# Feature-major products with hi and lo activations as one 512-column operand, halves summed in evacuation, one pool of eight PSUM banks

## The chip, the cores and the metric

The kernel runs on one core of one Trainium2 chip. The metric is the time of one execution on the device in microseconds. Three timed runs of the kernel before gave 1062.16, 1062.8 and 1064.5 us, so the median is 1062.8 us. The profile is of one more execution; the profiler's span, from its first to its last instruction, is 1060.4 us.

## The reference, cut to what matters

Two layers over 256 tokens of width 2048, in float32. Layer 0 is stick-breaking attention, layer 1 multi-head latent attention on keys and values made once from the residual stream.

```
# every layer: h = RMSNorm(x); y = W_out(mixer(h) * silu(gate(h))); x += RMSNorm(y)
#              x += (p[i] @ W_ple) * sigmoid(x @ W_gate)

def mixer_a(h, w_in, w_out):                       # 16 heads of 128
    q, k, v, g = jnp.split(h @ w_in, 4, axis=-1)   # w_in 2048 x 8192
    o = stick_breaking_attention(heads(q), heads(k), heads(v))
    return (o * jax.nn.silu(g)) @ w_out

def shared_kv(x, ...):                             # latent of 512, rotary key of 64
    ckv, k_rope = split(rms_norm(x) @ w_dkv); ckv = rms_norm(ckv)
    k_nope, v = ckv @ w_uk, ckv @ w_uv

def mixer_b(h, kv, w_in, ...):
    cq, g = jnp.split(h @ w_in, [512], axis=-1)    # g is 2048 wide
    q = rms_norm(cq) @ w_uq                        # per head 128 + 64 rotary
    return (mla_attention(q, k, v) * jax.nn.silu(g)) @ w_out
```

## The kernel before

Every product is done in float32r in two parts: an operand is split into `hi` (its float32r rounding, made by ScalarE, `split` and `split_gain`, lines 82 and 86) and `lo` (the rest, made by VectorE, lines 83 and 87). A product is the sum hi*hi + hi*lo + lo*hi, added up in PSUM; `mm3` (lines 108 to 111) issues these three matrix instructions.

Weights come in units of half a MiB (`unit`, line 89): one DMA into a `raw` buffer [128, 1024], then `whi` on ScalarE and `wlo` on VectorE. There are four buffers of each of the three.

There are two shapes of product. `rows` (token-major) keeps a 128-token block of the activations stationary and streams 512 columns of weights. `cols` (feature-major) keeps a 128x128 block of weights stationary and streams the activations of all 256 tokens. Per weight block and per 128 rows of the contraction, `cols` issues three instructions of 256 columns: `whi` with the activations' hi (L109), `whi` with their lo (L110), `wlo` with their hi (L111). Two blocks share a PSUM bank of 512 columns, the left and the right half.

Feature-major are the gates of mixer A (four groups of four heads, `gate_group` and the three groups written out ahead of it), queries and keys of mixer A (`group_a`, four groups each), the gates of mixer B (four groups) and the nope keys and queries of mixer B (`group_b`, on the latents `latT`, two units for each of both in each of four groups). A group of the first three kinds is 8 units of 8 (row block, weight block) steps, in two banks; a unit of the last kind is 8 such steps, in one bank.

A result leaves PSUM in one operation per bank: VectorE multiplies a bank by the row of 1/rms (`gate_out` line 221, `group_a` line 337), or copies it (`group_b` line 550). The gates then pass through ScalarE's Silu (line 223).

PSUM has eight banks. The pool has two tags: `acc`, four banks for the large products, and `att`, four banks for attention, transposes and the row of 1/rms (one gate group uses two of them as well).

The order on each engine is made when the kernel is built: a scheduler takes the program in the order in which it is written and orders the ready instructions of each engine. The attention of a group of heads is woven into the weight stream of the next group (`weave`): a head has three stages, two units apart. An engine then works through its own list in order.

`actT` tiles hold activations as [hi or lo, row block, token], so that hi and lo of one row block lie 16 KB apart. `latT` holds the two latents in the same way.

Of the kernel before, what the change touches and what calls it, by code (L numbers as in the profile page):

```python
# [46 lines left out]
def hybrid_trunk(ctx: ExitStack, tc: tile.TileContext, a: dict):  # L47
    """Token-major residual; activations that feed a product are kept feature-major, split into two
    float32r parts (hi + lo is the float32 value exactly). A product is hi*hi + hi*lo + lo*hi,
    summed in PSUM in float32."""  # L50
# [8 lines left out]
    def acc():  # L59
        return psum.tile([P, SLAB], F32, tag="acc", name="acc", bufs=4)  # L60

    def att():
        return psum.tile([P, SLAB], F32, tag="att", name="att", bufs=4)
# [5 lines left out]
    # ---------------------------------------------------------------- residual stream  # L69
# [10 lines left out]
    # ---------------------------------------------------------------- weights  # L80
# [8 lines left out]
    def unit(src, n=UNIT, gains=None, parts=1):  # L89
        """Half a MiB of weights, split; gains: a factor per row, for each equal part of the columns."""  # L90
# [45 lines left out]
    def weave(stream, jobs, at):  # L136
        """Runs the stream of weight units; the stages of jobs[i] come after at[i], at[i] + LAG, ... of them."""
# [9 lines left out]
    # ---------------------------------------------------------------- constants  # L147
# [37 lines left out]
    def rstd_of(ssq, n, name):  # L185
        """ssq [P, NT, m] -> (mean + eps) ** -0.5, [P, NT]."""
# [10 lines left out]
    def rstd_row(r):  # L197
        """[P, NT] per token -> the same row in every partition, twice: [P, 2, T]."""
# [13 lines left out]
    def gate_group(g, aT, sg, get, row):  # L212
        o = [acc(), acc()]
        for u in range(8):
            cols(o, aT, get(u), 2 * u, 2, GRP, NK)
        gate_out(g, o, sg, row)
# [20 lines left out]
    o0, o1 = [acc(), acc()], [acc(), acc()]  # L237
    warm_up(WARM)
    for u in range(8):
# [4 lines left out]
        cols(o0, hT, w, 2 * u, 2, GRP, NK)  # L244
# [3 lines left out]
    c2 = tmp.tile([P, 2 * P + CHUNK], F32, tag="e", name="c2", bufs=2)  # L248
    for u in range(8):
        cols(o1, hT, unit_ga(1, u), 2 * u, 2, GRP, NK)  # L250
# [5 lines left out]
    o2 = [att(), att()]  # L256
    for u in range(8):
        cols(o2, hT, unit_ga(2, u), 2 * u, 2, GRP, NK)
# [4 lines left out]
        if u == 4:  # L263
            rstd0 = rstd_of(ssq0, D, "rstd0")
            rrow0 = rstd_row(rstd0)
            gate_out(0, o0, sgA, rrow0)
            gate_out(1, o1, sgA, rrow0)
    gate_out(2, o2, sgA, rrow0)
# [13 lines left out]
    gate_group(3, hT, sgA, lambda u: unit_ga(3, u), rrow0)  # L282

    # ---------------------------------------------------------------- mixer A
# [6 lines left out]
    def finish_head(h, o, sg, yT):  # L291
        y = tmp.tile([P, T], F32, tag="t256", name="y", bufs=2)
# [3 lines left out]
    def weighted_v(v, hh, w):  # L296
        """o.T [d, t] = v.T @ w.T; w [key, (t over keys 0..127 | last t tile over keys 128..255)]."""
# [32 lines left out]
    def group_a(g, q, k, v):  # L330
        for dst, base, row in ((k, NG, rrow0), (q, 0, rrow0q)):
            o = [acc(), acc()]
            for u in range(8):
                cols(o, hT, unit(a["w_in_a"][(base + g) * 8 + u]), 2 * u, 2, GRP, NK)
# [338 lines left out]
```

## Time and profile before

| | before |
|---|---|
| median of 3 runs | 1062.8 us (1062.16 to 1064.5) |
| span of the profiled execution, first to last instruction | 1060.4 us |
| TensorE busy | 1052.8 us, 6699 matrix instructions |
| VectorE busy | 606.7 us, 823 instructions |
| ScalarE busy | 536.2 us, 780 instructions |
| DMA | 189.17 MB, 178 GB/s on the mean |
| granted TensorE clock | 0.999 of full speed |

A time is that of a whole execution; the profiled execution's own time, by the profile, is its span, and the median of the timed runs lies 2.4 us above it. "Busy" of TensorE is the union of its instructions' modelled intervals. Those intervals overlap: one 256-column instruction is shown 0.28 us long while the next one starts 0.12 us after it, so a sum of shown durations is no time, and what an instruction costs is read from one start to the next. Weight loads (PEld) run beside the instructions. On the other engines a shown duration is close to the step from one instruction to the next.

### The profile page before, as it was taken

The numbers are of one execution on the slowest core, as the hardware profiler recorded it, in microseconds if no ns is written. First come the engines' busy times: TensorE is split into PE (matmuls) and PEld (weight loads), VectorE is DVE, ScalarE is ACT, GpSimd is POOL, SyncE is SP. The second block draws the span as 40 slices with busy tenths as digits, with TensorE's granted clock in tenths as the row PEclk, the third lists the DMA queues.
The fourth block names the chain that finished last, engine by engine and source line by source line (L and its number), as shares of the span: only waits on it lengthen the run. The fifth ranks groups of instructions, "written<-read, shape, count | busy, mean of one in ns | idle before, by whom it ended". The sixth has DMA issues, their size and how long they took to land.

```text
span 1060.4 us, 16605 instructions
## 1 busy us (share of the span) xinstructions
PE 1052.8 (99%) x6699; PEld 952.9 (90%) x6699; DVE 606.7 (57%) x823; ACT 536.2 (51%) x780; POOL 6.8 (1%) x10
## 2 busy tenths in 40 slices
PE   8999999999999999999999999999999999999998
PEld 7999999989989988888888999999988978888888
DVE  7454444554545555556666575555676755558554
ACT  7544335445445446545555555555454454446442
POOL 0000000000000000000000000000000000000000
PEclk9999999999999999999999999999999999999999
DMA  8755555555555554564756476656533334665662
GB/s 329 281 176 182 180 185 182 169 162 174 162 163 174 171 179 149 178 207 145 225 178 188 130 245 194 181 183 191 172 119 121 120 120 139 205 184 193 210 212 79
DMA packets 55821, 189.17 MB, mean 178 GB/s; under 512 B 6208, under 2 KB 6976, under 8 KB 55744
## 3 DMA queue, kind: packets, MB, share of 16 engines
q1 hardware_dynamic: 55600, 188.09, 56.5%
q8 instruction: 52, 0.85, 0.3%
q14 instruction: 25, 0.20, 0.1%
q10 hardware_dynamic: 144, 0.02, 0.0%
HBM read 185.99 MB, written 2.10 MB: 177 GB/s over the span
## 4 chain that ended last, share of the span: by engine, by line
PE 98%; DMA 1%; DVE 0%; ACT 0%; SPq 0%; issue 0%
PE acc L109 29%; PE acc L111 29%; PE acc L110 29%; PE att L300 1%; PE att L110 1%; PE att L111 1%; PE att L109 1%; PE att L171 1%; PE att L301 1%; PE att L523 1%; PE att L519 1%; PE att L308 1%; PE att L522 1%; DMA raw<-in_w_in_a_dram 1%; PE att L539 0%; PE att L518 0%
## 5 line engine op out<-in xcount | busy, mean ns | idle before, releaser
L83 DVE TENSOR_TENSOR wlo<-raw,whi 128x1024 fp32r<-128x1024 f32 (+1 forms) x295 | 358.5, 1217 | 306.2 <-ACT whi L82 305.1
L82 ACT ACTIVATE whi<-raw 128x1024 fp32r<-128x1024 f32 (+1 forms) x295 | 310.8, 1054 | 345.7 <-PE acc L111 181.7
L111 PE MATMUL acc<-whi,actT 128*128 128x512 f32 (+2 forms) x736 | 278.2, 379 | 0.0
L109 PE MATMUL acc<-whi,actT 128*128 128x512 f32 (+2 forms) x736 | 277.6, 378 | 0.0
L110 PE MATMUL acc<-wlo,actT 128*128 128x512 f32 (+2 forms) x736 | 277.1, 377 | 0.0
L109 PE MATMUL acc<-actT,whi 128*128 128x256 f32 x960 | 272.8, 285 | 1.2 <-ACT whi L82 1.2
L110 PE MATMUL acc<-actT,whi 128*128 128x256 f32 x960 | 271.9, 284 | 0.0
L111 PE MATMUL acc<-actT,wlo 128*128 128x256 f32 x960 | 270.8, 283 | 0.5 <-DVE wlo L83 0.5
L109 PEld LDWEIGHTS acc<-actT,whi 128*128 128x128 f32 x960 | 184.1, 192 | 2.0 <-ACT whi L82 1.9
L111 PEld LDWEIGHTS acc<-actT,wlo 128*128 128x128 f32 x960 | 183.5, 192 | 0.9 <-DVE wlo L83 0.9
L110 PEld LDWEIGHTS acc<-actT,whi 128*128 128x128 f32 x960 | 184.1, 192 | 0.1
L111 PEld LDWEIGHTS acc<-whi,actT 128*128 128x128 f32 x736 | 138.3, 188 | 24.7 <-issue 0.7
L109 PEld LDWEIGHTS acc<-whi,actT 128*128 128x128 f32 x736 | 138.4, 188 | 24.4 <-issue 0.3
L110 PEld LDWEIGHTS acc<-wlo,actT 128*128 128x128 f32 x736 | 138.6, 188 | 24.1
L87 DVE SCALAR_TENSOR_TENSOR wlo<-raw,pre,whi 128x512 fp32r<-128x512 f32 x80 | 56.8, 748 | 41.6 <-ACT whi L86 41.6
L86 ACT ACTIVATE whi<-raw,pre 128x512 fp32r<-128x512 f32 x80 | 53.4, 716 | 49.8 <-PE acc L110 28.6
L109 PE MATMUL acc<-latT,whi 128*128 128x256 f32 x128 | 36.6, 290 | 0.2 <-ACT latT L86 0.2
L111 PE MATMUL acc<-latT,wlo 128*128 128x256 f32 x128 | 36.7, 289 | 0.0
L110 PE MATMUL acc<-latT,whi 128*128 128x256 f32 x128 | 36.2, 285 | 0.3 <-DVE latT L87 0.3
L111 PEld LDWEIGHTS acc<-latT,wlo 128*128 128x128 f32 x128 | 24.4, 191 | 1.3 <-issue 1.3
L109 PEld LDWEIGHTS acc<-latT,whi 128*128 128x128 f32 x128 | 24.3, 191 | 1.1 <-issue 0.7
L110 PEld LDWEIGHTS acc<-latT,whi 128*128 128x128 f32 x128 | 24.4, 191 | 0.5 <-DVE latT L87 0.5
(233 smaller groups left out, 944.2 us busy)
## 6 DMA issues: line engine op xcount, KB each, us to landing
raw<-in_w_in_a_dram SPq DMA_DIRECT2D x127, 512.0 KB, 3.6
raw<-in_w_in_b_dram SPq DMA_DIRECT2D x40, 512.0 KB, 4.2
raw<-in_w_out_a_dram SPq DMA_DIRECT2D x32, 512.0 KB, 3.7
raw<-in_w_pg_a_dram SPq DMA_DIRECT2D x32, 512.0 KB, 3.6
raw<-in_w_out_b_dram SPq DMA_DIRECT2D x32, 512.0 KB, 3.6
raw<-in_w_pg_b_dram SPq DMA_DIRECT2D x24, 512.0 KB, 3.6
raw<-in_w_dkv_dram SPq DMA_DIRECT2D x16, 288.0 KB, 2.8
raw<-in_w_pp_dram SPq DMA_DIRECT2D x8, 512.0 KB, 3.5
```

The lines of the kernel that those rows point to most:

```text
L82: nc.scalar.activation(hi, src, AF.Copy)
L83: nc.vector.tensor_tensor(lo, src, hi.bitcast(F32), ALU.subtract)
L86: nc.scalar.activation(hi, src, AF.Copy, scale=gain)
L87: nc.vector.scalar_tensor_tensor(lo, src, gain, hi.bitcast(F32), ALU.mult, ALU.subtract)
L109: nc.tensor.matmul(out, lhsT=sh, rhs=mh, start=start, stop=False, **kw)
L110: nc.tensor.matmul(out, lhsT=sh, rhs=ml, start=False, stop=False, **kw)
L111: nc.tensor.matmul(out, lhsT=sl, rhs=mh, start=False, stop=stop, **kw)
L171: nc.tensor.transpose(b[:, kk * T + t * P:kk * T + (t + 1) * P], x[:, t, k * P:(k + 1) * P], ident)
L300: nc.tensor.matmul(o, lhsT=v[:, 0, c], rhs=w[:, :T], start=True, stop=False)
L301: nc.tensor.matmul(o[:, P:], lhsT=v[:, 1, c], rhs=w[:, T:], start=False, stop=True)
L308: mm(z[:, :T], lhsT=k[:, hh, :P], rhs=q[:, hh, :], start=True, stop=False, skip_group_check=True)
L519: mm(s[:, P:], lhsT=q[:, hh, P:], rhs=k[:, hh, :], start=False, stop=False, skip_group_check=True)
```

## The change

`cols` issues two instructions in place of three. The activations are kept as [row block, hi or lo, token], so that hi and lo of one row block are 512 neighbouring columns. One instruction of 512 columns multiplies `whi` with both (L133): the left half of the bank collects hi*hi, the right half hi*lo. One of 256 columns adds `wlo` times hi to the left half (L135). The loop over the banks is now the outer one and that over the row blocks inside a unit the inner one. A weight block thus needs a bank of its own, and the two halves of the bank have to be added on the way out: `halves` copies the right half to SBUF on ScalarE (L142, three buffers) and adds it to the left half on VectorE (L143). The multiplication by 1/rms then works on SBUF in place (L236, L358), as does Silu (L237). A gate group needs four banks instead of two, a unit of `group_b` two instead of one. All banks are one tag of eight.

```diff
     def acc():
-        return psum.tile([P, SLAB], F32, tag="acc", name="acc", bufs=4)
+        return psum.tile([P, SLAB], F32, tag="bank", name="acc", bufs=8)
     def att():
-        return psum.tile([P, SLAB], F32, tag="att", name="att", bufs=4)
+        return psum.tile([P, SLAB], F32, tag="bank", name="att", bufs=8)
...
-    def cols(banks, aT, w, k0, nk, nblk, ktot):
+    def cols(banks, aT, w, k0, nk, ktot):
         hi, lo = w
-        for kk in range(nk):
-            k = k0 + kk
-            for i in range(nblk):
-                c = slice((kk * nblk + i) * P, (kk * nblk + i + 1) * P)
-                mm3(banks[i // 2][:, i % 2 * T:(i % 2 + 1) * T], hi[:, c], lo[:, c], aT[0][:, k, :], aT[1][:, k, :],
-                    k == 0 and i % 2 == 0, k == ktot - 1 and i % 2 == 1, skip_group_check=True)
+        n = len(banks)
+        for i, o in enumerate(banks):
+            for kk in range(nk):
+                k = k0 + kk
+                c = slice((kk * n + i) * P, (kk * n + i + 1) * P)
+                nc.tensor.matmul(o, lhsT=hi[:, c], rhs=aT[2][:, k].rearrange("p i t -> p (i t)"), start=k == 0,
+                                 stop=False, skip_group_check=True)
+                nc.tensor.matmul(o[:, :T], lhsT=lo[:, c], rhs=aT[0][:, k, :], start=False, stop=k == ktot - 1,
+                                 skip_group_check=True)
+
+    def halves(dst, banks):
+        for i, o in enumerate(banks):
+            b = tmp.tile([P, T], F32, tag="t256", name="half", bufs=3)
+            nc.scalar.copy(b, o[:, T:])
+            nc.vector.tensor_tensor(dst[:, i, :], o[:, :T], b, ALU.add)
...
     def act_t():
-        b = big.tile([P, 2, NK, T], F32R, tag="actT", name="actT", bufs=2)
-        return b[:, 0], b[:, 1]
+        b = big.tile([P, NK, 2, T], F32R, tag="actT", name="actT", bufs=2)
+        return b[:, :, 0, :], b[:, :, 1, :], b
...
-    def gate_out(g, o, sg, row):
+    def gate_out(g, sg, row):
         for i in range(2):
-            gt = tmp.tile([P, 2, T], F32, tag="t512", name="gt", bufs=2)
-            nc.vector.tensor_tensor(gt, pair(o[i]), row, ALU.mult)
-            h = g * GRP + 2 * i
-            silus.append(nc.scalar.activation(sg[:, h:h + 2, :], gt, AF.Silu))
+            h = sg[:, GRP * g + 2 * i:GRP * g + 2 * i + 2, :]
+            nc.vector.tensor_tensor(h, h, row, ALU.mult)
+            silus.append(nc.scalar.activation(h, h, AF.Silu))
...
     def group_a(g, q, k, v):
         for dst, base, row in ((k, NG, rrow0), (q, 0, rrow0q)):
-            o = [acc(), acc()]
+            o = banks4()
...
+            halves(dst, o)
             for i in range(2):
-                nc.vector.tensor_tensor(dst[:, 2 * i:2 * i + 2, :], pair(o[i]), row, ALU.mult)
+                d = dst[:, 2 * i:2 * i + 2, :]
+                nc.vector.tensor_tensor(d, d, row, ALU.mult)
...
     def group_b(g, q, qr, k, v):
...
-                o = acc()
-                cols([o], aT, unit(src[g * (GRP // 2) + i]), 0, NR, 2, NR)
-                nc.vector.tensor_copy(dst[:, 2 * i:2 * i + 2, :], pair(o))
+                o = [acc(), acc()]
+                cols(o, aT, unit(src[g * (GRP // 2) + i]), 0, NR, NR)
+                halves(dst[:, 2 * i:2 * i + 2, :], o)
```

What stands on TensorE where mixer A goes from the values of the first group to the keys of the second. The first row is the last instruction of `rows`; `acc` is a bank, `whi` and `wlo` the weights, `actT` the activations. Before:

```order
L111 MATMUL acc<-whi,actT 128x512
L109 MATMUL acc<-actT,whi 128x256 [waits Activation_49]
L110 MATMUL acc<-actT,whi 128x256
L111 MATMUL acc<-actT,wlo 128x256 [waits DVE_49]
L109 MATMUL acc<-actT,whi 128x256
L110 MATMUL acc<-actT,whi 128x256
L111 MATMUL acc<-actT,wlo 128x256
L109 MATMUL acc<-actT,whi 128x256 [waits PE_49]
```

And of the change, from the same row on:

```order
L111 MATMUL acc<-whi,actT 128x512
L133 MATMUL acc<-actT,whi 128x512
L135 MATMUL acc<-actT,wlo 128x256 [waits DVE_49]
L133 MATMUL acc<-actT,whi 128x512
L135 MATMUL acc<-actT,wlo 128x256
L133 MATMUL acc<-actT,whi 128x512 [waits PE_49]
```

Three instructions of 256 columns have become one of 512 and one of 256, and the first of a group waits neither for ScalarE nor for VectorE, so neither for a bank that they still read.

The second place is the entry of mixer B, on VectorE: the last gate group leaves PSUM and the latents (`latT`, in PSUM banks `att` after their transposes) are split. `gt` and `sgB` are the gates, `rrow` is the row of 1/rms, `c_383` and `c_331` the tile of constants, `arena` the keys of mixer B. Before:

```order
L83 TENSOR_TENSOR wlo<-raw,whi 128x1024 [waits DMAHW4_49,PE_49,Activation_49]
L221 TENSOR_TENSOR gt<-acc,rrow 128x512 [waits PE_49] x2
L83 TENSOR_TENSOR wlo<-raw,whi 128x1024 [waits DMAHW5_49,Activation_49]
L87 SCALAR_TENSOR_TENSOR latT<-att,c_383,latT 128x256 [waits Activation_49] x8
L550 COPY arena<-acc 128x512 [waits PE_49]
```

And of the change:

```order
L83 TENSOR_TENSOR wlo<-raw,whi 128x1024 [waits DMAHW4_49,PE_49,Activation_49]
L143 TENSOR_TENSOR sgB<-acc,half 128x256 [waits Activation_49] x3
L236 TENSOR_TENSOR sgB<-sgB,rrow 128x512 [waits DVE_49]
L83 TENSOR_TENSOR wlo<-raw,whi 128x1024 [waits DMAHW5_49,PE_49,Activation_49]
L143 TENSOR_TENSOR sgB<-acc,half 128x256 [waits Activation_49]
L87 SCALAR_TENSOR_TENSOR latT<-att,c_331,latT 128x256 [waits Activation_49] x2
L236 TENSOR_TENSOR sgB<-sgB,rrow 128x512 [waits DVE_49]
L87 SCALAR_TENSOR_TENSOR latT<-att,c_331,latT 128x256 [waits Activation_49] x6
```

One addition now stands between the weights' lo and the first split of the latents, and one multiplication after the second split.

ScalarE's list at the same place, before:

```order
L82 ACTIVATE whi<-raw 128x1024 [waits DMAHW5_49,DVE_49,PE_49]
L223 ACTIVATE sgB<-gt 128x512 [waits DVE_49]
L86 ACTIVATE latT<-att,c_383 128x256 [waits PE_49] x2
L223 ACTIVATE sgB<-gt 128x512 [waits DVE_49]
L86 ACTIVATE latT<-att,c_383 128x256 [waits PE_49] x2
```

And of the change:

```order
L142 COPY half<-acc 128x256 [waits PE_49] x3
L82 ACTIVATE whi<-raw 128x1024 [waits DMAHW5_49,DVE_49,PE_49]
L142 COPY half<-acc 128x256 [waits DVE_49,PE_49]
L86 ACTIVATE latT<-att,c_331 128x256 [waits PE_49] x2
L237 ACTIVATE sgB<-sgB 128x512 [waits DVE_49]
```

Three copies now stand ahead of the weights' hi and one behind it.

## Rows read from the trace of the kernel before

**Rows 1.** The page: span, TensorE's busy time, the chain by engine.

```profile
span 1060.4 us, 16605 instructions
PE 1052.8 (99%) x6699; PEld 952.9 (90%) x6699; DVE 606.7 (57%) x823; ACT 536.2 (51%) x780; POOL 6.8 (1%) x10
...
PE 98%; DMA 1%; DVE 0%; ACT 0%; SPq 0%; issue 0%
```

**Rows 2.** Waits of PE: what waited for what, us in total, times, longest.

```profile
PE acc L109 <- ACT whi L82: 1.2, 2, 0.6
PE acc L111 <- DVE wlo L83: 0.5, 1, 0.5
```

**Rows 3.** Groups by shape: the first of the three feature-major instructions, xcount, busy us.

```profile
L109 PE MATMUL acc<-actT,whi 128*128 128x256 f32 x960 | 272.8, 285 | 1.2 <-ACT whi L82 1.2
...
L109 PE MATMUL acc<-latT,whi 128*128 128x256 f32 x128 | 36.6, 290 | 0.2 <-ACT latT L86 0.2
...
L109 PE MATMUL att<-actT,whi 128*128 128x256 f32 x64 | 18.2, 284 | 0.0
```

**Rows 4.** Timeline of PE near 801 us: start, shown duration; first and 27th of a run.

```profile
799.84 0.28 PE L109 MATMUL acc<-latT,whi 128*128 128x256 f32 x1
...
802.96 0.28 PE L111 MATMUL acc<-latT,wlo 128*128 128x256 f32 x1
```

**Rows 5.** Timeline of PE near 560 us: first and eleventh of a 512-column run.

```profile
559.62 0.39 PE L111 MATMUL acc<-whi,actT 128*128 128x512 f32 x1
...
561.89 0.39 PE L109 MATMUL acc<-whi,actT 128*128 128x512 f32 x1
```

**Rows 6.** Timeline of PE at 146 and 168 us, where the widths change.

```profile
146.16 0.28 PE L111 MATMUL acc<-actT,wlo 128*128 128x256 f32 x1
146.28 0.40 PE L109 MATMUL acc<-whi,actT 128*128 128x512 f32 x1
...
167.84 0.39 PE L111 MATMUL acc<-whi,actT 128*128 128x512 f32 x1
168.07 0.28 PE L109 MATMUL acc<-actT,whi 128*128 128x256 f32 x1
```

**Rows 7.** Groups by shape on ACT and DVE: xcount, busy us, mean ns.

```profile
L481 ACT COPY krT<-att 128x256 f32<-128x256 f32 x1 | 0.3, 347 | 0.0
...
L86 ACT ACTIVATE latT<-att,c 128x256 fp32r<-128x256 f32 x8 | 3.1, 483 | 0.0
...
L293 DVE TENSOR_TENSOR y<-att,sgA 128x256 f32<-128x256 f32 x16 | 6.8, 424 | 15.3 <-PE att L301 15.3
...
L550 DVE COPY arena<-acc 128x512 f32<-128x512 f32 x16 | 11.0, 688 | 5.5 <-PE acc L111 5.5
```

**Rows 8.** Busy time in mixer B, stretch 739 to 870 us: PE, PEld, DVE, ACT, POOL, clock, DMA.

```profile
739.00:870.00 131.00, 130.56 (x873) 115.58 (x872) 88.79 (x196) 65.97 (x135) 0.00 (x0) 1.00 0.42 130
```

**Rows 9.** Timeline of ACT and of DVE near 141 us, in brackets idle before.

```profile
140.60 1.06 ACT L82 ACTIVATE whi<-raw 128x1024 fp32r<-128x1024 f32 x1 [1.82 <-PE acc L110]
...
141.69 1.23 DVE L83 TENSOR_TENSOR wlo<-raw,whi 128x1024 fp32r<-128x1024 f32 x1 [1.65 <-ACT whi L82]
```

**Rows 10.** Timelines of PE, ACT and DVE at the entry of mixer B.

```profile
737.62 1.91 PE L501 MATMUL att<-c,lat 128*128 128x128 f32 x16
737.70 1.06 ACT L82 ACTIVATE whi<-raw 128x1024 fp32r<-128x1024 f32 x1 [1.82 <-PE acc L110]
739.70 0.50 PE L109 MATMUL acc<-latT,whi 128*128 128x256 f32 x2 [0.16 <-ACT latT L86]
739.94 1.86 DVE L87 SCALAR_TENSOR_TENSOR latT<-att,c,latT 128x256 fp32r<-128x256 f32 x4
740.47 0.39 PE L110 MATMUL acc<-latT,whi 128*128 128x256 f32 x1 [0.28 <-DVE latT L87]
```

**Rows 11.** Timeline of PE at the start: last wait of the first gate group.

```profile
9.16 0.39 PE L109 MATMUL acc<-actT,whi 128*128 128x256 f32 x1 [0.63 <-ACT whi L82]
9.62 0.28 PE L110 MATMUL acc<-actT,whi 128*128 128x256 f32 x1
10.42 0.39 PE L111 MATMUL acc<-actT,wlo 128*128 128x256 f32 x1 [0.52 <-DVE wlo L83]
```

More of the change, by code (lines that the diff above doesn't have):

```diff
@@ L210, in hybrid_trunk, with banks4, gate_group @@
     silus = []
-    def gate_group(g, aT, sg, get, row):
-        o = [acc(), acc()]
+    def banks4():
+        return [acc() for _ in range(GRP)]
+    def gate_group(g, aT, sg, get):
+        o = banks4()
         for u in range(8):
-            cols(o, aT, get(u), 2 * u, 2, GRP, NK)
-        gate_out(g, o, sg, row)
-    def gate_out(g, o, sg, row):
+            cols(o, aT, get(u), 2 * u, 2, NK)
+        halves(sg[:, GRP * g:GRP * (g + 1), :], o)
+    def gate_out(g, sg, row):
         for i in range(2):
-            gt = tmp.tile([P, 2, T], F32, tag="t512", name="gt", bufs=2)
-            nc.vector.tensor_tensor(gt, pair(o[i]), row, ALU.mult)
-            h = g * GRP + 2 * i
-            silus.append(nc.scalar.activation(sg[:, h:h + 2, :], gt, AF.Silu))
+            h = sg[:, GRP * g + 2 * i:GRP * g + 2 * i + 2, :]
+            nc.vector.tensor_tensor(h, h, row, ALU.mult)
+            silus.append(nc.scalar.activation(h, h, AF.Silu))
     def warm_up(n):
@@ L236, in hybrid_trunk @@
     sgA = big.tile([P, NH, T], F32, tag="sg", name="sgA", bufs=1)
-    o0, o1 = [acc(), acc()], [acc(), acc()]
+    o = banks4()
     warm_up(WARM)
@@ L243, in hybrid_trunk @@
             split_gain(hT[0][:, k, :], hT[1][:, k, :], xs[:, k, :], pre[:, 0, k:k + 1])
-        cols(o0, hT, w, 2 * u, 2, GRP, NK)
+        cols(o, hT, w, 2 * u, 2, NK)
+    halves(sgA[:, :GRP, :], o)
     ssq0 = ssq_tile("ssq0")
@@ L248, in hybrid_trunk @@
     c2 = tmp.tile([P, 2 * P + CHUNK], F32, tag="e", name="c2", bufs=2)
+    o = banks4()
     for u in range(8):
-        cols(o1, hT, unit_ga(1, u), 2 * u, 2, GRP, NK)
+        cols(o, hT, unit_ga(1, u), 2 * u, 2, NK)
         if u in (1, 4, 7):
@@ L255, in hybrid_trunk @@
     ident = c1[:, :P]
-    o2 = [att(), att()]
+    halves(sgA[:, GRP:2 * GRP, :], o)
+    o = banks4()
     for u in range(8):
-        cols(o2, hT, unit_ga(2, u), 2 * u, 2, GRP, NK)
+        cols(o, hT, unit_ga(2, u), 2 * u, 2, NK)
         if u == 0:
@@ L265, in hybrid_trunk @@
             rrow0 = rstd_row(rstd0)
-            gate_out(0, o0, sgA, rrow0)
-            gate_out(1, o1, sgA, rrow0)
-    gate_out(2, o2, sgA, rrow0)
+            gate_out(0, sgA, rrow0)
+            gate_out(1, sgA, rrow0)
+    halves(sgA[:, 2 * GRP:3 * GRP, :], o)
+    gate_out(2, sgA, rrow0)
     rrow0q = tmp.tile([P, 2, T], F32, tag="rrow", name="rrow0q", bufs=2)
@@ L280, in hybrid_trunk @@
     nc.vector.tensor_copy(trir, c2[:, :P])
-    gate_group(3, hT, sgA, lambda u: unit_ga(3, u), rrow0)
+    gate_group(3, hT, sgA, lambda u: unit_ga(3, u))
+    gate_out(3, sgA, rrow0)
     W3 = T + P
@@ L291, in finish_head @@
     def finish_head(h, o, sg, yT):
-        y = tmp.tile([P, T], F32, tag="t256", name="y", bufs=2)
+        y = tmp.tile([P, T], F32, tag="t256", name="y", bufs=3)
         nc.vector.tensor_tensor(y, o, sg[:, h, :], ALU.mult)
@@ L331, in group_a @@
         for dst, base, row in ((k, NG, rrow0), (q, 0, rrow0q)):
-            o = [acc(), acc()]
+            o = banks4()
             for u in range(8):
-                cols(o, hT, unit(a["w_in_a"][(base + g) * 8 + u]), 2 * u, 2, GRP, NK)
+                cols(o, hT, unit(a["w_in_a"][(base + g) * 8 + u]), 2 * u, 2, NK)
                 yield
+            halves(dst, o)
             for i in range(2):
-                nc.vector.tensor_tensor(dst[:, 2 * i:2 * i + 2, :], pair(o[i]), row, ALU.mult)
+                d = dst[:, 2 * i:2 * i + 2, :]
+                nc.vector.tensor_tensor(d, d, row, ALU.mult)
         o = [acc(), acc()]
@@ L466, in rotate @@
         nc.vector.tensor_tensor(dst, src, cs, ALU.mult)
-        u = tmp.tile([P, GRP, ROPE], F32, tag="t256", name="rot", bufs=2)[:, :n, :]
+        u = tmp.tile([P, GRP, ROPE], F32, tag="t256", name="rot", bufs=3)[:, :n, :]
         for lo_, hi_ in ((0, hw), (hw, 0)):
@@ L471, in rotate @@
         nc.vector.tensor_tensor(dst, dst, u, ALU.add)
-    krt = tmp.tile([P, NT, 2, ROPE], F32, tag="t256", name="krt", bufs=2)
+    krt = tmp.tile([P, NT, 2, ROPE], F32, tag="t256", name="krt", bufs=3)
     for t in range(NT):
@@ L485, in hybrid_trunk @@
     for g in range(NG):
-        gate_group(g, x2T, sgB, lambda u: unit_b(1 + g, u), rrow2)
-    latT = big.tile([P, 2, 2, NR, T], F32R, tag="tok", name="latT", bufs=3)
+        gate_group(g, x2T, sgB, lambda u: unit_b(1 + g, u))
+        gate_out(g, sgB, rrow2)
+    latT = big.tile([P, 2, NR, 2, T], F32R, tag="tok", name="latT", bufs=3)
     for i, src in ((0, ckv), (1, cq)):
@@ L503, in hybrid_trunk @@
                 k = 2 * j + kk
-                split_gain(latT[:, i, 0, k, :], latT[:, i, 1, k, :], b[:, kk * T:(kk + 1) * T], qln[:, i, k:k + 1])
-    ckvT, cqT = [(latT[:, i, 0], latT[:, i, 1]) for i in range(2)]
+                split_gain(latT[:, i, k, 0, :], latT[:, i, k, 1, :], b[:, kk * T:(kk + 1) * T], qln[:, i, k:k + 1])
+    ckvT, cqT = [(latT[:, i, :, 0, :], latT[:, i, :, 1, :], latT[:, i]) for i in range(2)]
     yT = act_t()
```

## The prediction

> **What bounds the kernel now.** I read the page first: TensorE is busy for 1052.8 of 1060.4 us, and the chain that ended last is TensorE for 98% [rows 1]. A busy TensorE can hide small waits, so next came the list of what it waited for: its longest entries behind the weights are 1.2 us in two waits and 0.5 us in one [rows 2], all at the start of the first gate group, and the entry of mixer B adds some tenths [rows 10]. So the span is, but for some 3 us, the sum of TensorE's own steps from start to start. The third view is therefore the timeline of TensorE, for what one step costs. What the reader is to see there: 26 steps of 256 columns take 802.96 - 799.84 = 3.12 us, 120.0 ns each [rows 4], and ten steps of 512 columns take 2.27 us, 227 ns each [rows 5]. The step is not proportional to the columns: doubling them adds 107 ns, and 120 - 107 = 13 ns come with every instruction, whatever its width. Where the widths change, a 256 is followed by a 512 after 0.12 us and a 512 by a 256 after 0.23 us [rows 6]: the step belongs to the earlier instruction and is the same in mixed company.
>
> By the Trainium skill, page "TensorE: Matmul & The Clock Gate", section "Back-to-back issue gap", an isolated instruction costs N / 2.4 ns and a fixed 2.5 ns more. By it three 256-column steps and a 512 with a 256 differ by 2.5 ns, and the change would give 1152 x 2.5 = 2.9 us. The trace does not agree: its fixed part is 13 ns, with a weight load beside each instruction.
>
> **What it removes.** Each (row block, weight block) step of `cols` goes from three 256-column instructions, 3 x 120.0 = 360 ns [rows 4], to one of 512 and one of 256 columns, 227 + 120 = 347 ns [rows 4, 5]. The same columns are streamed, one instruction fewer: 13.0 ns. Counting one instruction of each trio gives 960 + 128 + 64 = 1152 steps [rows 3]. 1152 x 13.0 ns = 15.0 us. All of it lies on the path, since TensorE waits for nothing in these stretches. The readings have a resolution of 10 ns over 26 and ten steps, so 227 could be 226 or 228 and the pair 346 to 348: 13.8 to 16.1 us.
>
> **What it adds.** Evacuation. `halves` runs for each weight block: 64 of the gates and of mixer A's queries and keys (16 groups of four) and 32 of mixer B, 96 in all. No row has this copy into SBUF more than once: a plain copy of 256 columns from PSUM on ScalarE took 347 ns, a split of the same size 483 ns with what it overlaps [rows 7], so 96 cost 33 to 46 us of ScalarE. I take 0.42 us each, half way. The addition is like the product of a PSUM and an SBUF operand of 256 columns, 424 ns [rows 7]: 96 cost 41 us of VectorE, against which the 16 copies of mixer B at 688 ns, 11 us, go. The products with 1/rms stay, 32 before and after, only from SBUF. ScalarE goes from 536 to some 576 us, VectorE from 607 to some 637 us, both far from TensorE's 1053 [rows 1]. The fullest stage is mixer B: VectorE 88.8 and ScalarE 66.0 of 131 us [rows 8]. Its 32 additions in place of 16 copies add 13.6 - 11.0 = 2.6 us there, its 32 copies 13 us to ScalarE. Neither becomes the bound.
>
> What covers the evacuation is the lead of the split weights. ScalarE makes the `whi` of a unit as soon as TensorE has freed a buffer (idle 1.82 us for it), VectorE its `wlo`, done at 141.69 + 1.23 = 142.92 us, 2.3 us after ScalarE's start at 140.60 [rows 9]. With four buffers this unit is used three units later; a unit is 24 steps of 120 ns, 2.88 us, so it lies ready for 8.64 - 2.3 = 6.3 us. After the change a unit lasts 8 x 347 = 2.78 us and the lead is 6.0 us. At the end of a group VectorE has at most four additions and two products more to do ahead of a `wlo`, 4 x 0.42 + 2 x 0.69 = 3.1 us, where two products, 1.4 us, stood before. The lead holds; without it each group end would cost up to these 3.1 us. The weights' DMAs have to follow TensorE 4% faster; the DMA engines are 42% busy in this stage [rows 8].
>
> Banks. A group takes four of eight, and the next group the other four, less what attention holds. The outer loop over banks helps: within a unit a bank is finished 2 x 347 ns after the one before it, so the first bank of a group is free to be read 2.1 us before the group's end, and its copy and addition (0.84 us) are over before the next group starts. I price bank waits at 0.3 us in all, near the lower end of 0, because inside the mixers the trace shows no wait of TensorE at all; the upper end I set at 3 us, 0.1 us at each of the 32 ends of groups and units, since the trace's own waits for another engine's result show 0.16 and 0.28 us of idle time where they occur [rows 10].
>
> **Two places where little changes hands.** The start: TensorE waits for the second unit's hi until 9.16, issues four products and waits for its lo until 10.42 us [rows 11]. Now it has four products of 512 columns to fill this wait with, 4 x 0.227 in place of 4 x 0.12 us, 0.43 us more work done by 10.42. Against it, the 0.1 us that the first unit saves is lost in the wait for 9.16, though the sum above counts it: a gain of 0.3 us. The entry of mixer B: the transposes of the latents start at 737.62 and the first products wait, the first until 739.70 and the next with the lo until 740.47, 2.85 us after the transposes' start [rows 10]. TensorE needs hi and lo together now. ScalarE's hi of the weights ends 1.14 us after the transposes' start (737.70 + 1.06), the last copy at 1.6, the first latent's hi at 2.0; VectorE's list has the weights' lo (1.23 us from 1.2 on) and then the last addition, to 2.85, and the first lo at 3.3 us. So the first pair starts 3.3 us after the transposes' start, 1.6 us after their end at 1.74 (16 in 1.91 us, less the tail of the last). Before, two products of 0.12 us went out in a wait that ended at 2.85 us: 0.87 us lost. A loss of 0.7 us more. Later latents come in time, since each now feeds 4 x 0.347 us of work.
>
> **Sum.** -15.0 - 0.3 + 0.7 + 0.3 = -14.3 us on the span of 1060.4 us, 1046.1 us. The median of the runs lies 2.4 us above this span, and nothing outside the span changes: 1048.5 us.
>
> **Rivals.** (1) Late evacuation. Some waits appear in the mixers, at bank changes or behind additions that stand ahead of a `wlo` or of attention. For it: both engines' lists grow, and in mixer B VectorE is two thirds busy [rows 8]. Against it: a lead of 6 us. At 0.1 us for each of 96 evacuations it takes 9.6 us back: 1058. The Trainium skill, "Perfetto Trace Analysis", section "Optimization Strategy", says that the same gap repeating on the engine that should be saturated can mean too few PSUM buffers; no run here has shown it yet.
>
> (2) Slower: the banks run out. If the group just ended still held the banks that the next one needs, TensorE would stand for the whole chain of copies and additions: five times 0.42 us, 2.1 us, at 16 groups of four banks and 1.26 us at 16 units of two, 33.6 + 20.2 = 54 us: 1102 us. It decides from 15.0 / 54 = 28% of it on. Against it: the order of the change shows the first instruction of a new group with no wait for either reading engine.
>
> (3) The removed instruction was cheaper than its neighbours. It repeats the weights of the instruction before it; were its step 110 ns, 3 ns over the 107 ns of its columns, and that of the two others 125, the saving would be 1152 x 3 = 3.5 us, with the small terms 1059.7. Against it: 26 steps that mix all three kinds have no step that is off the 120 ns [rows 4]. The rule of the page above on the gap ends at the same place; by the row it is wrong here by 10 ns.
>
> (4) No effect: the 512 over hi and lo runs as two halves, 240 ns, and the trio's price stays: 1063. Against it: all 512s step by 227 ns [rows 5].
>
> **Chances.** Forecast, 1046 to 1050.5: 0.74. Rival 1: 0.13. Better than 1046: 0.03. Rivals 3 and 4: 0.03 each. Rival 2: 0.04. A difference of under 0.2%, 2.1 us, can't be told from none in this kernel. Faster: 0.74 + 0.13 + 0.03 + 0.03 = 0.93; same 0.03; slower 0.04. The range reaches from 1045.5, the pair at its lowest and no wait (1062.8 - 16.1 - 0.3 less the runs' spread of 0.6), to 1053, which takes in the upper ends (bank waits of 3 us, the pair at its highest) and a little of rival 1. The likeliest case's own range is 1046 to 1050.5.
>
> **What would show it.** Right: starts of L133 to L135 0.23 us apart and of L135 to L133 0.12 us; 1152 fewer TensorE instructions; TensorE busy down by about 15 us; ScalarE and VectorE up by some 40 and 30 us. The copy reads 0.35 to 0.48 us. Wrong: rows of idle before L133 or L135 in the list of waits, beyond the start and the entry of mixer B, or a pair that takes 360 ns.

## The result: slower by 0.7%, and the profile after

Four runs of the changed kernel gave a median of 1069.97 us (1069.19 to 1071.48), beside 1062.48 us for the kernel before (1062.15 to 1064.5): ratio 1.0072, 95% interval 1.0057 to 1.0086. The forecast was 1048.5 us. The profiled execution took 1069.19 us, its span 1067.4 us. The page of the changed kernel has, for [rows 1 and 3]:

```profile
span 1067.4 us, 14511 instructions
PE 1047.6 (98%) x5547; PEld 893.3 (84%) x5547; DVE 629.7 (59%) x903; ACT 564.4 (53%) x876; POOL 6.9 (1%) x10
...
PE 95%; DVE 2%; ACT 1%; DMA 0%; issue 0%; SPq 0%; ACTq 0%
...
L133 PE MATMUL acc<-actT,whi 128*128 128x512 f32 x1024 | 360.7, 398 | 0.1
L135 PE MATMUL acc<-actT,wlo 128*128 128x256 f32 x1024 | 282.8, 280 | 0.1
...
L142 ACT COPY half<-acc 128x256 f32<-128x256 f32 x96 | 34.2, 363 | 18.9 <-PE acc L135 18.8
```

The 1152 instructions are gone and TensorE is busy for 5.2 us less, but the span is 7.0 us longer. The chain now holds 2% of VectorE and 1% of ScalarE where TensorE had 98%: it waits. The list of TensorE's waits (us in total, times, longest) names for whom. Of these rows, only the wait for `latT` has a counterpart before the change, 0.28 us in [rows 10]:

```profile
PE att L183 <- DVE x L437: 7.5, 4, 2.4
PE att L561 <- DVE pr L556: 1.8, 1, 1.8
PE acc L133 <- DVE latT L87: 1.8, 2, 1.3
...
PE att L319 <- ACT pT__6947 L563: 1.0, 1, 1.0
PE att L319 <- ACT pT__7605 L563: 1.0, 1, 1.0
PE att L319 <- ACT pT__7276 L563: 1.0, 1, 1.0
```

The largest row is in code that the diff touches only through the tag of `att`: the transposes of x (L183; L171 in the kernel before) behind each gate slab of layer 0, `between`. A slab's result passes ScalarE (sigmoid), two products and two sums on VectorE (one of each for each half of the tokens), and then x is transposed. The timeline of all engines at the first of the four places, after:

```profile
520.24 0.39 PE L111 MATMUL acc<-whi,actT 128*128 128x512 f32 x1
...
520.32 1.08 ACT L435 ACTIVATE sig<-acc 128x512 f32<-128x512 f32 x2
520.95 1.29 DVE L436 TENSOR_TENSOR sig<-sig,pp 128x512 f32<-128x512 f32 x2 [0.68 <-ACT sig L435]
...
522.16 1.29 DVE L437 TENSOR_TENSOR x<-x,sig 128x512 f32<-128x512 f32 x2
...
522.99 0.41 PE L183 MATMUL att<-c,x 128*128 128x128 f32 x2 [2.36 <-DVE x L437]
```

And of the kernel before at the same slab:

```profile
527.92 0.39 PE L111 MATMUL acc<-whi,actT 128*128 128x512 f32 x1
528.00 1.09 ACT L414 ACTIVATE sig<-acc 128x512 f32<-128x512 f32 x2
...
529.84 1.29 DVE L416 TENSOR_TENSOR x<-x,sig 128x512 f32<-128x512 f32 x2
...
534.72 1.03 PE L171 MATMUL att<-c,x 128*128 128x128 f32 x8
```

The chain from the slab's end to x takes some 3 us in both. Before, TensorE worked on the next slab meanwhile and came to the transposes 6.8 us after the slab's end, 3.6 us after x was done. After the change, the first two of the eight transposes are the next thing on TensorE's list, and everything behind them stands still: 2.75 us from start to start in place of 0.23. At the next two slabs it is 2.5 us, at the last 1.26. The order made at the build shows it (after, TensorE, the same place):

```
L109 MATMUL acc<-whi,actT 128x512
L110 MATMUL acc<-wlo,actT 128x512
L111 MATMUL acc<-whi,actT 128x512
L183 MATMUL att<-c_331,x 128x128 [waits DVE_49,PE_49]
L183 MATMUL att<-c_331,x 128x128
L109 MATMUL acc<-whi,actT 128x512 [waits Activation_49]
```

A second loss follows the third of these waits. The timeline of TensorE there, and the row of the stretch 573 to 577 us (length; busy time of PE, PEld, DVE, ACT, POOL; granted clock, DMA share, GB/s), after:

```profile
573.05 0.41 PE L183 MATMUL att<-c,x 128*128 128x128 f32 x2 [2.11 <-DVE x L437]
573.22 0.51 PE L109 MATMUL acc<-whi,actT 128*128 128x512 f32 x1
573.53 0.63 PE L110 MATMUL acc<-wlo,actT 128*128 128x512 f32 x1
573.95 0.63 PE L111 MATMUL acc<-whi,actT 128*128 128x512 f32 x1
574.38 0.63 PE L109 MATMUL acc<-whi,actT 128*128 128x512 f32 x1
```

```profile
573.00:577.00 4.00, 3.95 (x12) 3.17 (x13) 1.64 (x2) 1.38 (x4) 0.00 (x0) 0.57 0.40 129
```

Steps of 427 ns where [rows 5] has 227: the granted clock is at its lower level, 1.2 GHz, for eight steps, 1.6 us more.

To place the difference I took TensorE's steps, start to start, and subtracted a nominal price: columns at 2.4 GHz and 13.4 ns for an instruction of 256 columns or more (120 and 227 ns, [rows 4, 5]), the median of its kind for a narrower one. What is left, in us, by stage:

| stage (times of before) | before | after | pools apart | late x | before, one pool | heads spread |
|---|---|---|---|---|---|---|
| start, gates A, first k and q (to 146) | 1.9 | 3.8 | 3.8 | 3.3 | 1.6 | 3.5 |
| mixer A (to 435) | 8.0 | 8.8 | 8.8 | 8.8 | 8.0 | 8.9 |
| output product and gate slabs of layer 0 (to 596) | 0.3 | 10.1 | 0.3 | 1.2 | 11.7 | 1.2 |
| entry of mixer B (738 to 763) | 1.0 | 2.6 | 1.4 | 2.4 | 1.0 | 2.5 |
| mixer B (to 897) | 13.0 | 19.7 | 14.4 | 18.2 | 16.9 | 14.9 |
| span | 1060.4 | 1067.4 | 1049.8 | 1056.2 | 1076.9 | 1051.8 |

(The last four columns are runs below; the stages left out hold under 0.3 us each.) Between before and after these rows grow by 20.8 us, and the span by 7.0. The 13.8 us between the two are no measurement of the gain: the nominal price already takes 13.4 ns off for each of the 1152 instructions. What the form gained is read from runs that share the arrangement of the banks and differ in the form (medians, runs below): with one pool 1078.67 and 1069.97 us, with one pool and late x 1068.37 and 1058.55, with pools apart 1062.18 and 1051.89. That is 8.7, 9.8 and 10.3 us, where the forecast had 14.3 for the form with all that it adds. The gain is there, smaller than forecast, and the waits take it back and more.

### The profile page after: what moved, and what is told of

The parts are those of the page before. It is cut to its first block, busy times and chain, and to the rows that moved or that the text cites. A ratio compares the mean times of both kernels' runs of the same rounds, so it can differ in the third digit from the quotient of the medians.

```text
span 1067.4 us, 14511 instructions
## 1 busy us (share of the span) xinstructions
PE 1047.6 (98%) x5547; PEld 893.3 (84%) x5547; DVE 629.7 (59%) x903; ACT 564.4 (53%) x876; POOL 6.9 (1%) x10
## 4 chain that ended last, share of the span: by engine, by line
PE 95%; DVE 2%; ACT 1%; DMA 0%; issue 0%; SPq 0%; ACTq 0%
PE acc L133 25%; PE acc L109 16%; PE acc L110 16%; PE acc L111 16%; PE acc L135 13%; PE att L319 1%; PE att L183 1%; PE att L545 1%; PE att L541 1%; PE att L327 1%; PE att L544 1%; PE att L320 1%; DVE wlo L83 1%; DMA raw<-in_w_in_a_dram 0%; DVE sig L436 0%; ACT whi L82 0%
## 5 line engine op out<-in xcount | busy, mean ns | idle before, releaser
L133 PE MATMUL acc<-actT,whi 128*128 128x512 f32 x1024 | 360.7, 398 | 0.1
L135 PE MATMUL acc<-actT,wlo 128*128 128x256 f32 x1024 | 282.8, 280 | 0.1
L133 PEld LDWEIGHTS acc<-actT,whi 128*128 128x128 f32 x1024 | 191.9, 188 | 43.0 <-ACT whi L82 1.1
L135 PEld LDWEIGHTS acc<-actT,wlo 128*128 128x128 f32 x1024 | 193.3, 189 | 2.4 <-DVE wlo L83 0.5
L133 PE MATMUL acc<-latT,whi 128*128 128x512 f32 x128 | 48.0, 414 | 1.8 <-DVE latT L87 1.8
L142 ACT COPY half<-acc 128x256 f32<-128x256 f32 x96 | 34.2, 363 | 18.9 <-PE acc L135 18.8
L135 PE MATMUL acc<-latT,wlo 128*128 128x256 f32 x128 | 36.7, 287 | 0.0
L133 PEld LDWEIGHTS acc<-latT,whi 128*128 128x128 f32 x128 | 24.7, 193 | 8.8 <-DVE latT L87 2.3
L553 ACT ACTIVATE pr<-att,st 128x128 f32<-128x128 f32 (+1 forms) x32 | 13.2, 418 | 24.3 <-DVE st L551 24.3
L135 PEld LDWEIGHTS acc<-latT,wlo 128*128 128x128 f32 x128 | 24.9, 194 | 0.3 <-issue 0.3
L82 ACT ACTIVATE actT<-y 128x256 fp32r<-128x256 f32 x32 | 13.5, 422 | 17.1 <-DVE y L312 16.8
L109 PE MATMUL acc<-whi,latT 128*128 128x256 f32 (+1 forms) x64 | 22.2, 347 | 0.0
```

The costliest lines, as they stand in the source:

```text
L82: nc.scalar.activation(hi, src, AF.Copy)
L109: nc.tensor.matmul(out, lhsT=sh, rhs=mh, start=start, stop=False, **kw)
L133: nc.tensor.matmul(o, lhsT=hi[:, c], rhs=aT[2][:, k].rearrange("p i t -> p (i t)"), start=k == 0, stop=False, skip_group_check=True)
L135: nc.tensor.matmul(o[:, :T], lhsT=lo[:, c], rhs=aT[0][:, k, :], start=False, stop=k == ktot - 1, skip_group_check=True)
L142: nc.scalar.copy(b, o[:, T:])
L553: nc.scalar.activation(pr[:, c], s[:, c], AF.Exp, scale=SCALE_B, bias=st[:, 1, t:t + 1], accum_out=st[:, 2, t:t + 1])
```

## The experiments

My theory from here on, ORDER: the single pool of eight banks, not the two-instruction form, lets the build place transposes right behind what they depend on. The first four runs part this from the form (FORM) and from the layout.

**Pools apart: the changed kernel with four banks `acc` and four `att` again.**

```diff
-        return psum.tile([P, SLAB], F32, tag="bank", name="acc", bufs=8)
+        return psum.tile([P, SLAB], F32, tag="acc", name="acc", bufs=4)
...
-        return psum.tile([P, SLAB], F32, tag="bank", name="att", bufs=8)
+        return psum.tile([P, SLAB], F32, tag="att", name="att", bufs=4)
```

> The changed kernel with its eight banks parted again as before, four called acc and four att; layout, two-instruction form and halves stay. Theory ORDER (the one pool lets the build place transposes right behind the work they depend on, and TensorE then waits for VectorE and ScalarE): the 9.8 us of idle steps around the four gate slabs of layer 0 and the 6.7 us more in mixer B go back to what they were before, so about 1054 to 1056 us (1070.0 less 9.8, 6.7 and up to 1.6 at the entry of mixer B, with up to 2 us for groups that now find only four banks). Theory FORM (the 512-column form itself, or its way out through ScalarE and VectorE, costs the time): it stays at 1066 us or above.

Measured: 1051.89 us (1051.01 to 1052.21), ratio 0.9900 to the kernel before (0.9887 to 0.9914), 2 us under the range of ORDER. In the order the eight transposes of a slab stand some 30 products behind its end again, and in TensorE's list of waits L183, L561 and L319 are gone:

```profile
PE acc L133 <- DVE arena L143: 1.2, 2, 0.6
PE att L243 <- DVE zeros L161: 1.2, 1, 1.2
PE acc L133 <- ACT whi L82: 0.7, 1, 0.7
PE acc L133 <- DVE sgA L143: 0.5, 1, 0.5
```

What came in are three waits for a bank that `halves` still read (`arena`, `sgA`: 1.7 us), the price of four banks. FORM is out.

**Late x: one pool, the transposes of x written later.** `after_gate` of a slab of layer 0 runs after the third weight unit of the next slab.

```diff
         for u in range(nu):
+            if u == LATE and pend:
+                pend.pop()()
...
-            after_gate(cs)
+            if i == 0:
+                pend.append(lambda cs=cs: after_gate(cs))
+            else:
+                after_gate(cs)
```

> The changed kernel, one pool of eight, with the eight transposes of x behind each gate slab of layer 0 written three weight units later in the program (36 products behind the slab's end instead of right at it); nothing else moves. Theory ORDER: the waits of 2.5 us at three of the four slabs go, and with them the half-clock stretch at 573 us: 1070.0 less 8 to 9 is 1061 to 1062 us, mixer B unchanged. Theory FORM: the time that VectorE and ScalarE take is lost anyway, a wait of the same size shows later, 1068 to 1070 us.

Measured: 1058.55 us (1057.97 to 1058.83), ratio 0.9964 (0.9952 to 0.9977), 11.4 us under the changed kernel, more than expected. The half-clock stretch at 573 us went too. Of the waits for x only the last slab's stayed, at 0.9 us:

```profile
PE att L570 <- DVE pr L565: 1.8, 1, 1.8
...
PE att L183 <- DVE x L441: 0.9, 1, 0.9
```

Mixer B lost 18.2 us, 1.5 less than in the changed kernel, where ORDER had expected no change. The wait for `pr` is as long as there, but the lower clock that followed it there (0.61 from 774 to 778 us) did not come: from 763 to 767 us the granted clock was 1.00.

**Before with one pool: the three-instruction form, and only the two tags `acc` and `att` made one of eight, as in the change.**

> The kernel before, with its three-instruction form and its layout, and only the eight banks made one pool. Theory ORDER: this alone brings the waits at the slabs of layer 0 (about 9 us) and some of those in mixer B (up to 7): 1070 to 1078 us. Theory FORM: 1062.5 us, as before.

Measured: 1078.67 us (1077.06 to 1079.23), ratio 1.0149 (1.0135 to 1.0163), just over the range of ORDER. The pool alone costs 16.5 us of span and brings the waits for x and for pT to the old form (not the one for `pr`):

```profile
PE att L171 <- DVE x L416: 7.5, 4, 2.4
...
PE att L300 <- ACT pT__8453 L541: 1.1, 1, 1.1
```

**Before with the new layout: hi and lo side by side.**

```diff
-        b = big.tile([P, 2, NK, T], F32R, tag="actT", name="actT", bufs=2)
-        return b[:, 0], b[:, 1]
+        b = big.tile([P, NK, 2, T], F32R, tag="actT", name="actT", bufs=2)
+        return b[:, :, 0, :], b[:, :, 1, :]
```

> The kernel before, and only the activations' hi and lo laid side by side for each k instead of in two halves of the tile; order of instructions as before. Theories ORDER and FORM: 1062.5 us within 0.2%. Theory LAYOUT (reading or writing the interleaved tile is slower): over 1065 us.

Measured: 1062.3 us, ratio 1.0002 (0.9993 to 1.0011). The layout by itself costs and gives nothing that can be told from zero.

The next two ask whether each place pays for its own sharing. Both add a tag of two banks and leave six to the rest (`acc` and `att`).

**Mixers apart, and x apart.** In the first, the attention's tiles of both mixers take the two banks; in the second, the transposes of x do.

```diff
-        return psum.tile([P, SLAB], F32, tag="bank", name="att", bufs=8)
+        return psum.tile([P, SLAB], F32, tag="bank", name="att", bufs=6)
+
+    def mix():
+        return psum.tile([P, SLAB], F32, tag="mix", name="att", bufs=2)
...
```

> The changed kernel with two of the eight banks kept for the attention tiles of both mixers (z, s, the transposed pr, weighted_v) and six shared by everything else, the transposes of x with them. In the order of instructions the first two transposes behind each gate slab of layer 0 stand right at the slab's end, as in the changed kernel. Theory SHARING (a tile that shares its pool with acc comes early, each place for itself): the waits of about 9.8 us around those slabs stay, mixer B loses only what it did with the pools apart (14.4 us against 19.7): 1063 to 1066 us. Rival THEORY MIXERS (the attention's share of the pool is the root, the rest follows): 1052 to 1055 us.

Measured: 1065.62 us (1064.52 to 1068.5), ratio 1.0039 (1.0026 to 1.0053). TensorE waits for x four times, 7.2 us in all; mixer B is at 15.6 us.

> The mirror of that: two banks kept for the transposes of x alone, six shared by all else, the attention's tiles with them; the transposes stand 32 to 36 products behind the slab's end. Theory SHARING: the waits at the slabs of layer 0 go, mixer B stays at 18 to 20 us: 1055 to 1060 us. Rival MIXERS: no gain beside the changed kernel, 1068 to 1071 us.

Measured: 1062.36 us (1061.11 to 1065.66), ratio 1.0007 (0.9998 to 1.0017), 2 us over the expected range. The waits for x are gone and mixer B stays at 19.1 us, as SHARING says; what the range had left out is the price of two banks for x: two new waits of 1.3 us together (for `wlo`, behind the transposes ahead of the gate slabs, one in each layer), and at the entry of mixer B 3.3 us where the changed kernel has 2.6. These are read from an execution of 1061.13 us at a granted clock of 1.000; that of 1065.66 us had 0.995, so part of the median is a lower clock that no profile here shows:

```profile
PE acc L136 <- DVE latT L90: 2.5, 2, 1.3
PE att L564 <- DVE pr L559: 1.8, 1, 1.8
PE acc L113 <- DVE wlo L86: 1.3, 2, 0.7
```

So each place goes with the banks that it takes itself; the two losses are separate.

**Six and two, five and three banks** in the diff of the first run, in place of four and four.

> The changed kernel with pools apart, six banks acc and two att instead of four and four. Theory BANKS (what the four-and-four version still loses at bank changes, three waits of TensorE of 1.7 us together for VectorE's sums, is the want of a fifth and sixth acc bank): these waits go, 1050 us, ratio 0.988 to 0.990. Rival ATT (two banks are too few for the attention's tiles, whose chain through ScalarE and VectorE then shows): 1055 us or more.

Measured: 1056.87 us, ratio 0.9950 (0.9937 to 0.9962).

> The same with five and three. BANKS: half of the 1.7 us goes, 1050 to 1051.5 us. ATT: 1053 us or more.

Measured: 1053.27 us, ratio 0.9916 (0.9903 to 0.9930). BANKS fell as a way to more speed: the waits for `arena` and `sgA` did go, but with two `att` banks others came, 2.1 us for the first latents and 2.4 us behind transposes of x (six and two):

```profile
PE acc L133 <- DVE latT L87: 2.1, 1, 2.1
PE acc L110 <- DVE wlo L83: 1.3, 2, 0.7
...
PE att L109 <- DVE actT L83: 1.1, 1, 1.1
```

With five and three the first is gone, and the last stays at 1.1 us.

**Before with one pool and late x**, the edits of the second and third run together.

> The kernel before with the eight banks as one pool (1078.7 us in its own run) and, as in the late-transposes run, the transposes of x behind each gate slab of layer 0 written three weight units later; the three-instruction form stays. Theory ORDER: the place of the transposes costs the same whatever the form of the feature products, so about 11 us come back: 1066 to 1069 us. Rival (the gain of the late place belongs to the two-instruction form): 1075 us or more.

Measured: 1068.37 us (1068.0 to 1068.91), ratio 1.0059 (1.0047 to 1.0072): 10.3 us back of 16.5. The place has nearly the same price (11.4) under the new form.

**Double copy**, on the version with pools apart:

```diff
             nc.scalar.copy(b, o[:, T:])
+            nc.scalar.copy(b, o[:, T:])
```

> The four-and-four version (1051.9 us) with the copy of a bank's upper half made twice by ScalarE, 96 more instructions of 0.36 us, 34 us of ScalarE's time. Theory HIDDEN (the way out of the banks lies beside TensorE's work): 1051 to 1053 us. Rival PATH (the next use of the bank waits for it): about 0.36 us for each of some 16 to 28 changes of group that follow at once, 1058 to 1062 us.

Measured: 1055.81 us (1055.24 to 1057.64), ratio 0.9942 (0.9930 to 0.9955). Between the two: the second copies raise ScalarE's busy time from 564.5 to 589.6 us, by 25 us and not 34, and cost 3.9 us. TensorE waits 2.1 us for `sgA` (0.5 before), and the excess grows by 2.0 us up to the end of the first k and q and by 1.1 in mixer A. The way out of a bank is mostly, not wholly, covered when a group has four banks of its own and no more.

**Other banks**: second k and second q product of a group of mixer B in `att` banks.

```diff
-                o = [acc(), acc()]
+                o = [acc(), acc()] if i == 0 else [att(), att()]
                 cols(o, aT, unit(src[g * (GRP // 2) + i]), 0, NR, NR)
```

> The four-and-four version with the second k and the second q product of each group of mixer B in att banks instead of acc. Theory BANKS: the two waits of about 1 us in mixer B for VectorE's sums go, 1050 to 1051 us. Rival ATT (the attention's tiles now wait for their banks, or the order turns against it as in the shared pool): 1053 us or more.

Measured: 1051.26 us (1050.89 to 1051.5), ratio 0.9897 (0.9884 to 0.9911). The two waits for `arena` are gone, one of 0.5 us for ScalarE's pT came. The interval overlaps that of pools apart; with 0.3 us less span I count it as the same, though its median is the lowest here.

**k outside**: the loop over the banks inside again.

```diff
-        for i, o in enumerate(banks):
-            for kk in range(nk):
+        for kk in range(nk):
+            for i, o in enumerate(banks):
```

> The four-and-four version with the loop over k outside again and the banks inside, as before the change, so that the four banks of a unit end within its last four pairs. Theory BANKS: the first bank is then free later by about three pairs (1 us) when the next group begins, 3 to 6 us more over the group changes, 1055 to 1058 us. Rival (two pairs of slack are enough for ScalarE and VectorE): 1051 to 1053 us.

Measured: 1053.59 us (1052.8 to 1054.39), ratio 0.9919 (0.9906 to 0.9933): 1.7 us over pools apart, less than BANKS said and more than its rival allowed. The new order of loops is worth these 1.7 us with four banks, in the first stage (6.3 in place of 3.8 us).

So far the loss in mixer B had gone only with a parting of the pools. The last two runs move the order there and keep one pool.

**Heads spread**, on late x:

```diff
...
-        weave(group_b(g, q, qr, k, v), jobs, (1, 3, 5, 6))
+        weave(group_b(g, q, qr, k, v), jobs, (0, 1, 2, 3), 3)
```

(The numbers are the units at which the four heads begin; the 3 is how many units apart a head's stages stand, 2 before.)

> The one-pool version with the late transposes (1058.6 us), and in mixer B the stages of a head put three weight units apart instead of two, its four heads beginning at units 0, 1, 2, 3 instead of 1, 3, 5, 6: a head's transposes then stand 27 to 32 products behind its scores (21 before), and no head's six transposes stand right ahead of its weighted values. All eight banks stay one pool. Theory PLACE: the waits of 1.8 us for VectorE's pr and of 3 times 1.0 us for ScalarE's pT go, with the half-clock stretch behind the first: 1053 to 1056 us. Rival BANKS SHARED (the attention's tiles wait for banks that the products hold): waits of the same size show elsewhere in mixer B, 1057 to 1060 us.

Measured: 1053.58 us (1052.82 to 1054.58), ratio 0.9918 (0.9904 to 0.9931). Mixer B falls from 18.2 to 14.9 us. The wait for `pr` is gone, and those for pT are 0.3 us each:

```profile
PE att L183 <- DVE x L441: 0.9, 1, 0.9
...
PE att L319 <- ACT pT__7249 L572: 0.3, 1, 0.3
```

**Last slab too**, on heads spread: its transposes written behind the sixth w_dkv unit (`rest` holds the call that writes them).

```diff
...
 for k in range(NK):
+        if k == 6:
+            rest.pop()()
         hi, lo = unit(a["w_dkv"][k], RANK + ROPE, gains=[kvn[:, k:k + 1]])
```

> The same, and the transposes behind the last gate slab of layer 0 written behind the sixth of the sixteen w_dkv units. PLACE: the last wait for x, 0.9 us, goes as well: about 1 us under the run before. Rival: no difference.

Measured: 1052.58 us (1052.07 to 1053.7), ratio 0.9907 (0.9894 to 0.9921), 1.0 us less, and the row for L183 is gone. So with eight shared banks and only the places of instructions changed, the loss is regained to within 0.7 us of the version with pools apart. It is the place of the instructions (PLACE), in both parts.

## Why the prediction was wrong

**What bounds the kernel: right.** TensorE's steps set the span before, and so each wait put into them shows in full.

**What the change removes: right in kind, too large in size.** A run of 489 alternating instructions in the gates of mixer B goes from 651.88 to 736.55 us, 347.0 ns a pair (forecast 347):

```profile
651.88 0.36 PE L135 MATMUL acc<-actT,wlo 128*128 128x256 f32 x1
...
736.55 0.28 PE L135 MATMUL acc<-actT,wlo 128*128 128x256 f32 x1
```

That is one run. In the longest of layer 0, from 70 to 143 us, a pair takes 353 to 354 ns. With pools apart it is the other way round, 349 ns in layer 0 (65.59 to 142.99 us) and 353 in the gates of mixer B (383 steps):

```profile
661.90 0.48 PE L133 MATMUL acc<-actT,whi 128*128 128x512 f32 x1
...
729.49 0.28 PE L135 MATMUL acc<-actT,wlo 128*128 128x256 f32 x1
```

So the price is not one of the layer, and the 347 in that one run is partly luck. Over all feature-major steps within 40 ns of their nominal price, three instructions took 359.7 ns before and a pair takes 349.9 ns after: 9.8 ns and not 13.0, 11.3 us over the 1152 steps and not 15.0. What failed in this term is that a step "is the same in mixed company": in alternation the 512 takes 233 ns on the mean and the 256 takes 117, where [rows 6] had shown one change of width each way. Rival 3 (3.5 us) and rival 4 (none) are refuted by these steps. (Two sums of the prediction are 0.3 us off: by its own terms the range begins at 1045.8, and rival 3 gives 1060.0.)

**What it adds: nearly right.** The copy takes 363 ns (0.42 us assumed, 347 ns the nearest row), the sum 416 to 419 ns (424). ScalarE is busy for 28 us more and VectorE for 23 (40 and 30). Both lie beside TensorE's work with eight banks; with four, the double copy shows that they are not wholly covered.

**Banks: this is the step that failed.** The sentence was "I price bank waits at 0.3 us in all, near the lower end of 0, because inside the mixers the trace shows no wait of TensorE at all". No wait for a bank that ScalarE or VectorE still read did come into the list. But the one pool was priced only as a supply of banks, and its other effect, on where the build places instructions, had no term in the sum. I compared the order at two places, both where the diff changes code. At the gate slabs of layer 0 and in the attention of mixer B the code is the same and the order is not, and the trace of before could not show a wait that its own order avoided. It did have the price: the chain from a slab's end to x takes some 3 us, at four slabs up to 12. Measured: 9.8 us more at the slabs (7.5 of waits and 1.6 of the lower clock in it) and 6.7 in mixer B, 16.5 of the 21.5 us by which the forecast was missed. In the old form the pool alone costs 16.5 us of span, 11.4 of it at the slabs.

**The start and the entry of mixer B.** At the entry the first pair starts 739.85 - 736.67 = 3.2 us after the transposes (forecast 3.3), but a second wait of 0.5 us for a later latent follows: 1.6 us lost instead of 0.7. At the start a gain of 0.3 us was forecast; the stage lost 1.9 us more than before instead; 384 of its pairs at some 6 ns over 347 are enough for that.

**Rival 1** had waits "at bank changes or behind additions that stand ahead of a `wlo` or of attention", 9.6 us and a time of 1058: too little beside the 16.5 us lost at the two places, which are others than it named, and for another reason. The rule named there, from the Trainium skill, "Perfetto Trace Analysis", "Optimization Strategy", is that the same gap repeating on the engine that should be saturated can mean too few PSUM buffers. Here the measurement differs: the gap of 2.5 to 2.75 us that repeats at the slabs came with the larger pool and went when the same banks were parted in four and four. The rule says "can", and these runs show a gap with another cause. **Rival 2**, the only one with the right sign, had the wrong cause: no bank ran out.

**What stays open.** Why the build puts the transposes earlier when they share a pool with the products was not traced; shown is that it does, in both forms, and what it costs. It may be the sharing itself or the number of banks that are free to a transpose: in every run where the order was early they had six or eight banks to draw on, in every run where the pools were parted four or fewer, and no run parts the two. Nor does any run explain why a pair takes 347 ns in one run of instructions and 353 in another.

## What to carry to other kernels

Merging buffer pools can be an edit of the order, not only of the supply: compare the order on the saturated engine over the whole program, above all in code that the diff leaves alone, and look for an instruction that now stands directly behind the end of the work it depends on. Price it by the chain between the two, read from the old trace. When a change has a sure gain and the time goes the other way, look for waits in untouched code first: here the form was worth 1%, and putting the pools back was all it needed.

## What the hardware showed unexpectedly

The clock fell after some waits and not after others of the same length. Behind the waits that ended at 522.99 and 548.02 us the 512-column steps stayed at 0.23 us; behind the one at 573.05 the granted clock was 0.57 of full speed over the next 4 us, with eight steps of 427 ns. It fell again behind the 1.8 us wait for `pr` that ended at 773 us:

```profile
774.00:778.00 4.00, 4.00 (x14) 3.10 (x15) 2.24 (x8) 1.21 (x5) 0.00 (x0) 0.61 0.44 135
```

In the kernel before with one pool, with the same four waits for x, it fell behind the first (0.59 from 531 to 535 us) and the second (0.57 from 558 to 562) and not behind the third (1.00 from 584 to 590); in late x it did not fall behind the wait for `pr`. So the length of a wait did not tell here whether the clock would fall.

A 512-column step in alternation with one of 256 takes 230 to 241 ns and the 256 one 112 to 120, though [rows 4, 5] have 227 and 120 among their own kind. The pair of the two takes 347 ns in some long runs and 353 in others of the same kernel.
